# A two-block transformer kernel: output weights' loads put behind the input weights' loads, and the norm's transposes moved by one token tile

## The chip, the cores and the metric

The kernel runs on one core of a Trainium2 chip. Its engines are TensorE (PE, the matmuls), VectorE (DVE), ScalarE (ACT), GpSimd (POOL) and SyncE (SP, which here only issues loads); each works through its own instructions in order and waits for the others by semaphores. The metric is the device time of one execution in microseconds. "Faster" and "slower" are told from the median of several runs.

## The reference

The input is one sequence of 512 tokens of width 1024, in fp32. The first block has two layers: softmax attention with a forget gate, and then a differential attention on shared keys and values. Each is followed by a convolutional feed-forward part:

```python
def _conv_ffn(x, w_in, conv_w, conv_b, w_out):
    u = x @ w_in
    up = jnp.pad(u, ((0, 0), (CONV_WIDTH - 1, 0), (0, 0)))
    u = sum(conv_w[j] * up[:, j:j + s] for j in range(CONV_WIDTH)) + conv_b
    g, val = u[..., :D_FF], u[..., D_FF:]
    return (jax.nn.silu(g) * val) @ w_out
x = _layer_norm(DN_ALPHA * x + h, ...)       # after the attention
x = _layer_norm(DN_ALPHA * x + f, ...)       # after the feed-forward part
...
```

The second block normalises x (RMS norm), runs a grouped-query attention beside a state-space branch, mixes both through `w_out_2`, adds and normalises again, and ends with a gated feed-forward part of the same width (2816) and without the convolution: `(silu(gate) * up) @ w_down`.

## The kernel before

Every fp32 operand is split into a high and a low part, and each product is three matmuls (high x high, high x low, low x high). Tokens are held in four tiles of 128. A scheduler orders the instructions of each engine at build time; the order is fixed after that.

Weights come in chunks of 128 x 1024 (`wchunk`, L170): SP loads one (512 KB, L183) into one of three `raw` buffers, ACT makes the high part `whi` (L185), DVE the low part `wlo` (L186), each in one of four buffers.

The feed-forward part (`st_out`) runs three times: ffn0 (about 272 to 623 us), ffn1 (887 to 1250) and ffn2 (1738 to 2085). `w_in(g)` multiplies x by one group of input weights (four chunks), applies the convolution (L835, L837, L846) and the gate; `st_load` (L1403) loads four 512 KB pieces of output weights into `wr` buffers (L1410, five buffers); `st_phase` multiplies with them in the manner of Strassen. The loop is: load for phase g, `w_in(g + 2)`, phase g, `w_in(g + 3)`. While `w_in(1)` runs, the program also issues loads of constants for the stage that follows, on POOL's queue: in ffn0 four for the differential attention (`ropecos`, `ropesin`, `blockmask`, then `lam`), in ffn1 thirteen for the second block (L1039 to L1053, L168, L878). Small operations on these constants (L661, L663, L1041, L1047, L881) stand on DVE and ACT among the convolution's operations. In ffn2 there are none.

The last rows of the output weights are multiplied by `xs`, tile by tile; at each tile's end the epilogue does the residual and the norm (L390, L372 to L381; before the second block also L1596, L1600), and hands the transposes of the normed tile to `later`. `need(t - depth)` then emits those that are due. A transpose turns a tile in eight 128 x 128 steps (L330; after `w_out_2` L1510), and the result is split again into `xTh` (L193, ACT) and `xTl` (L194, DVE), the operands of the next stage. The three places where this happens are called A (end of ffn0, next the value projection of the differential attention), B (end of ffn1, next the keys and queries of the second block) and C (end of `w_out_2`, next ffn2). At C the norm's steps are L1341, L1347, L1349 and L1353, and the first products of ffn2 take 256 tokens at a time, so `need` asks for two tiles ahead of each half:

```python
            for t0 in (0, 256):
                self.need(t0 // P + 1)
                for i in range(2):
                    for p, c in zip(ps[i], (gc, vc)):
                        self.ws_mm(p, c, i * P, self.xh, self.xl, t0, t0 + 256)
```

Of the kernel before, what the change touches and what calls it, by code (L numbers as in the profile page):

```python
# [17 lines left out]
P = 128  # L18
# [62 lines left out]
class K:  # L81
# [90 lines left out]
    def wchunk(self, src):  # L172

        nc = self.nc
        srcs = src if isinstance(src, list) else [src]
        nk, cols = srcs[0].shape[0] // P, sum(a.shape[1] for a in srcs)
        assert nk * cols <= 1024
        raw = self.wp.tile([P, 1024], F32, tag="raw", name="raw", bufs=3)[:, :nk * cols]
        hi = self.wp.tile([P, 1024], F32R, tag="whi", name="whi", bufs=4)[:, :nk * cols]
        lo = self.wp.tile([P, 1024], F32R, tag="wlo", name="wlo", bufs=4)[:, :nk * cols]  # L180
        c = 0
        for a in srcs:
            nc.sync.dma_start(raw.rearrange("p (k c) -> p k c", k=nk)[:, :, c:c + a.shape[1]], a.rearrange("(k p) c -> p k c", p=P))  # L183
            c += a.shape[1]
        nc.scalar.activation(hi, raw, AF.Copy)  # L185
        nc.vector.tensor_tensor(out=lo, in0=raw, in1=hi.bitcast(F32), op=ALU.subtract)  # L186
        return hi.rearrange("p (k c) -> p k c", k=nk), lo.rearrange("p (k c) -> p k c", k=nk)
# [177 lines left out]

    def layer_norm(self, t, G, B, jk):

        nc = self.nc
        x = self.x[:, t, :]
        nm = self.sm.tile([P, 2], F32, tag="nm", name="nm")  # L370
        vs = self.sm.tile([P, 2], F32, tag="vs", name="vs")
        nc.vector.tensor_reduce(out=nm[:, 0:1], in_=self.sums[t][:, :self.ns], axis=AX.X, op=ALU.add)  # L372
        nc.vector.tensor_scalar(out=nm[:, 1:2], in0=nm[:, 0:1], scalar1=-1.0 / (32 * D), scalar2=None, op0=ALU.mult)
        for i in range(2):
            nc.scalar.activation(jk, x[:, i * 512:(i + 1) * 512], AF.Square, scale=1.0 / 32, bias=nm[:, 1:2], accum_out=vs[:, i:i + 1])
        nc.vector.tensor_scalar(out=nm[:, 0:1], in0=nm[:, 0:1], scalar1=-1.0 / D, scalar2=None, op0=ALU.mult)
        nc.vector.scalar_tensor_tensor(out=x, in0=x, scalar=nm[:, 0:1], in1=G, op0=ALU.add, op1=ALU.mult)
        r = self.rstd2(vs, LN_EPS)
        for i in range(2):
            h = slice(i * 512, (i + 1) * 512)  # L380
            nc.vector.scalar_tensor_tensor(out=x[:, h], in0=x[:, h], scalar=r, in1=B[:, h], op0=ALU.mult, op1=ALU.add)  # L381

# [31 lines left out]
    def fox(self, pool):  # L414
# [35 lines left out]
        def oproj(half, post=None):  # L450
            self.out_proj(I["a_w_out"][0], half * 4, 4, lambda k: oT[half * 4 + k][0], lambda k: oT[half * 4 + k][1],
                          1.0 if half else ALPHA, post)
# [32 lines left out]
        for h in range(17):  # L485
# [11 lines left out]
            if h == 15:  # L497
                oproj(0)
        G, B = self.bcast(I["ln_attn_g"][0], "Pt", pool, 1280, 2), self.bcast(I["ln_attn_b"][0], "Pt", pool, 1280, 2)
        oproj(1, self.norm_post(G, B, pool.tile([P, S], F32, tag="NC", name="NC")))  # L500

# [25 lines left out]
    def qk_stack1(self, qp, kp, pool, Ck, buf, e, scale=-0.125):  # L527
        nc = self.nc
        A = pool.tile([P, S], F32R, tag=f"A{e}", name="A", bufs=2)
        B = pool.tile([P, S], F32R, tag=f"B{e}", name="B", bufs=2)  # L530
        Cc = Ck[e][buf]
        m, o = (slice(0, 64), slice(64, 128)) if e == 0 else (slice(64, 128), slice(0, 64))
        nc.scalar.activation(A[m], qp[m], AF.Copy, scale=scale)
        nc.vector.scalar_tensor_tensor(out=A[o], in0=qp[m], scalar=scale, in1=A[m].bitcast(F32), op0=ALU.mult, op1=ALU.subtract)
        nc.scalar.activation(B[m], kp[m], AF.Copy)
        nc.scalar.activation(B[o], kp[m], AF.Copy)
# [695 lines left out]
    def block2(self, bpool):  # L1232
        nc, I, tc = self.nc, self.I, self.tc
        W = I["w_in_2"][0]
# [32 lines left out]
        with tc.tile_pool(name="L", bufs=self.NL) as self.L:  # L1267
# [31 lines left out]
            with tc.tile_pool(name="mix", bufs=1) as pool:  # L1299
# [6 lines left out]
                for t in range(NT):  # L1306
# [7 lines left out]
                    for g in range(2):  # L1314
# [4 lines left out]
                        k, s = slice(g * 4, g * 4 + 4), slice(t * P, (t + 1) * P)  # L1319
# [19 lines left out]
                def epi(c, t, ps):  # L1339
# [3 lines left out]
                    if c == 1:  # L1343
# [10 lines left out]
                        self.later(t, lambda: self.to_T2(mo[t], t))  # L1354
                        for i in range(2):
                            nc.gpsimd.dma_start(xd[t, i], x[t][i])
                self.depth = 1
                for c in range(2):
                    self.xs(I["w_out_2"][0], c * 512, 512, KD, lambda k: mx[k][0], lambda k: mx[k][1], lambda t, ps, c=c: epi(c, t, ps), stagger=4 if c else 0)
        with tc.tile_pool(name="ffn2", bufs=1) as pool:  # L1360
# [1 line left out]

    NL = 38
    F0 = 1
    depth = 1

    @staticmethod
    def steps(gen, n):
# [108 lines left out]
    def st_out(self, pool, W, x, fresh, w_in, last, WR=5):  # L1477

        hs = {}
        Q = [pool.tile([P, 2, 512], F32, tag="Q", name="Q", bufs=4) for _ in range(4)]  # L1480

        def group(g, R):
            if g < 8:
                hs[g] = self.st_operands(pool, R)
            else:
                hs[g] = [pool.tile([P, self.BLOCKS], F32R, tag=n, name=n, bufs=3)[:, :1024] for n in ("hh", "hl")]
                self.split(R[:, :1024], *hs[g])

        for g in range(2):
            group(g, w_in(g))  # L1490
        for g in range(0, 8, 2):
            B = self.st_load(pool, W, g, WR)
            R = w_in(g + 2)
            self.st_phase(pool, B, (hs[g], hs[g + 1]), Q, x, g == 0, fresh and g == 0, WR)
            group(g + 2, R)
            R = w_in(g + 3)
            if g == 6:
                self.st_final(Q, x, fresh)
            group(g + 3, R)
        group(10, w_in(10))  # L1500
        op = lambda i: lambda k: hs[8 + k // 2][i][:, k % 2 * 512:(k % 2 + 1) * 512]
        epis = last()
        for c in range(2):
            self.xs(W, c * 512, 512, 6, op(0), op(1), epis(c), k0=16, stagger=3 * c, banks=3 * (1 - c))
# [129 lines left out]
```

## Time and profile before

| | |
|---|---|
| median of 3 runs | 2103.84 us (2103.47 to 2104.33) |
| profiled execution | 2104.43 us |
| its span | 2102.6 us, so 1.8 us lie around it |
| granted TensorE clock, mean | 0.992 |
| busy: PE, DVE, ACT, POOL | 2045.3, 1556.9, 1085.2, 77.5 us |
| chain that ended last | PE 80%, DVE 7%, ACT 7%, issue 3%, POOL 2%, DMA 2% |

PE is busy for 97% of the span. Since a busy engine may run at a lower clock, the granted clock is read beside it: 1.00 is 2.4 GHz, 0.5 is 1.2 GHz, and a window that holds both shows a value between. An idle time in square brackets stands in front of the row that ended it, with the row or transfer that PE waited for.

### The profile page before, as it was taken

Reading aid. Unit: us, or ns where it says so; the run is one execution under the profiler, and the core shown is the slowest. Engines: PE = TensorE matmul, PEld = TensorE weight load, DVE = VectorE, ACT = ScalarE, POOL = GpSimd, SP = SyncE. Lnnn points to the kernel's source line nnn. Section 1 sums busy time; section 2 is a strip of 40 time slices with the busy share of each in tenths; the row PEclk is TensorE's granted clock in tenths of the full one; section 3 lists DMA queues with packets and bytes.
Section 4 is the critical chain, followed back from the end, with each engine's and each line's share of the span. In section 5 each row is a group of like instructions: output and inputs, shape, how many; then the busy total and the mean of one; then the engine's idle time right before and its main releaser. Section 6 shows DMA issues by size and latency. Waiting matters only on the chain.

```text
span 2102.6 us, 28049 instructions
## 1 busy us (share of the span) xinstructions
PE 2045.3 (97%) x10563; PEld 1729.3 (82%) x10563; DVE 1556.9 (74%) x2776; ACT 1085.2 (52%) x1905; POOL 77.5 (4%) x113
## 2 busy tenths in 40 slices
PE   8999999999999999999999999999999999999998
PEld 7888888888878789888888877877898878888886
DVE  6777878788966888767887867897798545575564
ACT  4777655444435977445444443677476334443322
POOL 0000000000000000110000002000000001000000
PEclk9999999999999999999999999999999999999999
DMA  6222243233223221153223323211323425333222
GB/s 169 62 61 61 71 138 103 78 101 120 83 88 91 61 78 53 58 145 110 80 91 110 110 91 96 68 32 44 106 59 88 145 90 191 101 100 99 82 80 90
DMA packets 197469, 193.71 MB, mean 92 GB/s; under 512 B 8933, under 2 KB 170454, under 8 KB 197334
## 3 DMA queue, kind: packets, MB, share of 16 engines
q1 hardware_dynamic: 191398, 173.04, 27.5%
q0 software_dynamic: 5504, 17.31, 2.8%
q8 instruction: 83, 1.36, 0.3%
q10 hardware_dynamic: 432, 1.57, 0.2%
q14 instruction: 52, 0.43, 0.1%
HBM read 185.61 MB, written 6.29 MB: 91 GB/s over the span
## 4 chain that ended last, share of the span: by engine, by line
PE 80%; DVE 7%; ACT 7%; issue 3%; POOL 2%; DMA 2%; POOLq 0%; DVEq 0%; SPq 0%; ACTq 0%
PE mm L219 15%; PE mm L217 15%; PE mm L218 15%; PE at L1439 3%; PE at L1440 3%; PE at L1438 3%; PE mm L291 3%; PE mm L293 3%; PE mm L292 3%; PE at L401 2%; ACT sw L699 1%; DVE wlo L186 1%; PE mm L257 1%; PE mm L259 1%; PE mm L258 1%
## 5 line engine op out<-in xcount | busy, mean ns | idle before, releaser
L217 PE MATMUL mm<-xTh,whi 128*128 128x512 f32 (+1 forms) x1584 | 606.9, 383 | 4.7 <-ACT whi L185 3.3
L219 PE MATMUL mm<-xTh,wlo 128*128 128x512 f32 (+1 forms) x1584 | 605.5, 383 | 2.6 <-DVE wlo L186 2.6
L218 PE MATMUL mm<-xTl,whi 128*128 128x512 f32 (+1 forms) x1584 | 605.3, 382 | 0.0
L185 ACT ACTIVATE whi<-raw 128x1024 fp32r<-128x1024 f32 (+3 forms) x282 | 293.0, 1043 | 311.0 <-PE mm L218 172.7
L186 DVE TENSOR_TENSOR wlo<-raw,whi 128x1024 fp32r<-128x1024 f32 (+3 forms) x282 | 337.2, 1199 | 141.5 <-ACT whi L185 135.6
L217 PEld LDWEIGHTS mm<-xTh,whi 128*128 128x128 f32 x1584 | 299.6, 189 | 60.2 <-ACT whi L185 3.7
L219 PEld LDWEIGHTS mm<-xTh,wlo 128*128 128x128 f32 x1584 | 299.2, 189 | 59.4 <-DVE wlo L186 3.7
L218 PEld LDWEIGHTS mm<-xTl,whi 128*128 128x128 f32 x1584 | 299.6, 189 | 55.2 <-DVE xTl L194 0.2
L837 DVE SCALAR_TENSOR_TENSOR cy<-mm,cols,cy 128x511 f32<-128x511 f32 (+1 forms) x172 | 128.3, 746 | 69.7 <-ACT cy L835 67.6
L193 ACT ACTIVATE whi<-wr 128x1024 fp32r<-128x1024 f32 x84 | 89.0, 1060 | 90.2 <-PE mm L218 29.1
L835 ACT ACTIVATE cy<-mm,cols 128x512 f32<-128x512 f32 x86 | 66.5, 773 | 105.5 <-PE mm L219 105.5
L291 PE MATMUL mm<-whi,xTh 128*128 128x256 f32 x416 | 119.0, 287 | 0.8 <-ACT xTh L193 0.5
L292 PE MATMUL mm<-wlo,xTh 128*128 128x256 f32 x416 | 118.5, 285 | 0.4 <-DVE wlo L186 0.4
L293 PE MATMUL mm<-whi,xTl 128*128 128x256 f32 x416 | 118.5, 285 | 0.2 <-DVE xTl L194 0.2
L194 DVE TENSOR_TENSOR wlo<-wr,whi 128x1024 fp32r<-128x1024 f32 x84 | 102.0, 1221 | 12.9 <-ACT whi L193 12.1
L193 ACT ACTIVATE hh<-R 128x256 fp32r<-128x256 f32 (+2 forms) x57 | 54.9, 964 | 82.9 <-DVE R L1528 42.3
L1439 PE MATMUL at<-wlo,hh 128*128 128x512 f32 x240 | 93.4, 389 | 0.0
L1440 PE MATMUL at<-whi,hl 128*128 128x512 f32 x240 | 93.4, 389 | 0.0
L1438 PE MATMUL at<-whi,hh 128*128 128x512 f32 x240 | 92.7, 389 | 0.0
L193 ACT ACTIVATE ph<-at 128x512 fp32r<-128x512 f32 (+3 forms) x128 | 58.7, 474 | 53.8 <-PE at L401 40.3
L291 PEld LDWEIGHTS mm<-whi,xTh 128*128 128x128 f32 x416 | 80.1, 193 | 2.3 <-ACT xTh L193 1.0
L292 PEld LDWEIGHTS mm<-wlo,xTh 128*128 128x128 f32 x416 | 80.3, 193 | 1.6 <-DVE wlo L186 0.6
(451 smaller groups left out, 3860.9 us busy)
## 6 DMA issues: line engine op xcount, KB each, us to landing
raw<-in_ffn_w_in_dram SPq DMA_DIRECT2D x88, 512.0 KB
raw<-in_w_gate_up_dram SPq DMA_DIRECT2D x44, 512.0 KB
raw<-in_w_in_dram SPq DMA_DIRECT2D x40, 512.0 KB
wr<-in_ffn_w_out_dram SPq DMA_DIRECT2D x32, 512.0 KB
raw<-in_a_w_in_dram SPq DMA_DIRECT2D x22, 512.0 KB
raw<-in_kv_w_dram SPq DMA_DIRECT2D x16, 512.0 KB
wr<-in_w_down_dram SPq DMA_DIRECT2D x16, 512.0 KB
raw<-in_ffn_w_out_dram SPq DMA_DIRECT2D x12, 512.0 KB
```

What stands on the lines that cost most here:

```text
L185: nc.scalar.activation(hi, raw, AF.Copy)
L186: nc.vector.tensor_tensor(out=lo, in0=raw, in1=hi.bitcast(F32), op=ALU.subtract)
L193: nc.scalar.activation(hi, src, AF.Copy)
L217: mm(o, wh, a, start=(k == 0), stop=False)
L218: mm(o, wh, b, start=False, stop=False)
L219: mm(o, wl, a, start=False, stop=(k == ktiles - 1))
L291: mm(o, a, hi[:, kk, :], start=(k == 0 and t % 2 == 0), stop=False)
L292: mm(o, a, lo[:, kk, :], start=False, stop=False)
L293: mm(o, b, hi[:, kk, :], start=False, stop=(k == ktiles - 1 and t % 2 == 1))
L1438: mm(ps[t], a, wh, start=p == 0, stop=False)
L1439: mm(ps[t], a, wl, start=False, stop=False)
L1440: mm(ps[t], b, wh, start=False, stop=p == 1)
```

## The change

It has two parts. `wchunk` keeps the load that it issued last, and the four loads of a phase's output weights are issued after it, so they stand behind the last chunk of the input weights asked for so far. And `depth` is 2 in place of 1, for all three places: the transposes of tile t come at the end of tile t + 2 in place of t + 1.

```diff
--- before.py
+++ after.py
@@ -180,7 +180,7 @@
         lo = self.wp.tile([P, 1024], F32R, tag="wlo", name="wlo", bufs=4)[:, :nk * cols]
         c = 0
         for a in srcs:
-            nc.sync.dma_start(raw.rearrange("p (k c) -> p k c", k=nk)[:, :, c:c + a.shape[1]], a.rearrange("(k p) c -> p k c", p=P))
+            self.last_load = nc.sync.dma_start(raw.rearrange("p (k c) -> p k c", k=nk)[:, :, c:c + a.shape[1]], a.rearrange("(k p) c -> p k c", p=P)).ins
             c += a.shape[1]
         nc.scalar.activation(hi, raw, AF.Copy)
         nc.vector.tensor_tensor(out=lo, in0=raw, in1=hi.bitcast(F32), op=ALU.subtract)
@@ -1354,7 +1354,6 @@
                         self.later(t, lambda: self.to_T2(mo[t], t))
                         for i in range(2):
                             nc.gpsimd.dma_start(xd[t, i], x[t][i])
-                self.depth = 1
                 for c in range(2):
                     self.xs(I["w_out_2"][0], c * 512, 512, KD, lambda k: mx[k][0], lambda k: mx[k][1], lambda t, ps, c=c: epi(c, t, ps), stagger=4 if c else 0)
         with tc.tile_pool(name="ffn2", bufs=1) as pool:
@@ -1362,7 +1361,7 @@
 
     NL = 38
     F0 = 1
-    depth = 1
+    depth = 2
 
     @staticmethod
     def steps(gen, n):
@@ -1489,7 +1488,8 @@
         for g in range(2):
             group(g, w_in(g))
         for g in range(0, 8, 2):
-            B = self.st_load(pool, W, g, WR)
+            with self.tc.issue_after(self.last_load):
+                B = self.st_load(pool, W, g, WR)
             R = w_in(g + 2)
             self.st_phase(pool, B, (hs[g], hs[g + 1]), Q, x, g == 0, fresh and g == 0, WR)
             group(g + 2, R)
```

The order of SP's loads at the beginning of ffn0, before (-) and after (+); `raw` holds input weights, `wr` output weights:

```order
 L183 DMA raw<-in_a_w_out_dram 128x2x512 x4
-L183 DMA raw<-in_ffn_w_in_dram 128x4x256 x7
-L1410 DMA wr<-in_ffn_w_out_dram 128x2x512 x4
 L183 DMA raw<-in_ffn_w_in_dram 128x4x256 x8
-L1410 DMA wr<-in_ffn_w_out_dram 128x2x512 x4
+L1409 DMA wr<-in_ffn_w_out_dram 128x2x512 x4
```

The eighth load of input weights, the last chunk of `w_in(1)`, now stands ahead of the first four of output weights (the line number of these moves by one); ffn1 and ffn2 change in the same way, and every later group as well.

The order on DVE at place B, from the second norm's scaling of tile 0 (L1600) on, before:

```order
L1600 SCALAR_TENSOR_TENSOR Q<-x,ss_11344,wr 128x512 x2
L377 SCALAR_TENSOR_TENSOR x<-x,nm,wr 128x1024
L1381 SCALAR_TENSOR_TENSOR ss_11377<-vs 128x1
L194 TENSOR_TENSOR xTl<-at,xTh 128x4x128
L381 SCALAR_TENSOR_TENSOR x<-x,ss_11378,wr 128x512 x2
L194 TENSOR_TENSOR xTl<-at,xTh 128x4x128
L1381 SCALAR_TENSOR_TENSOR ss_11388<-ss_11385 128x1
L1600 SCALAR_TENSOR_TENSOR Q<-x,ss_11389,wr 128x512 x2
L390 SCALAR_TENSOR_TENSOR x,sums<-x,at 128x512
```

and after:

```order
L1600 SCALAR_TENSOR_TENSOR Q<-x,ss_11344,wr 128x512 x2
L377 SCALAR_TENSOR_TENSOR x<-x,nm,wr 128x1024
L1380 SCALAR_TENSOR_TENSOR ss_11377<-vs 128x1
L390 SCALAR_TENSOR_TENSOR x,sums<-x,at 128x512
L381 SCALAR_TENSOR_TENSOR x<-x,ss_11378,wr 128x512 x2
L372 TENSOR_REDUCE nm<-sums 128x1
L194 TENSOR_TENSOR xTl<-at,xTh 128x4x128
L373 TENSOR_SCALAR nm<-nm 128x1
L194 TENSOR_TENSOR xTl<-at,xTh 128x4x128
```

L377 and L381 are the first norm of the next tile, L194 the splits of a transposed tile. Before, tile 0's two splits stood in front of tile 2's residual (L390); now this residual stands in front of the splits, and so on for the following tiles.

The order on ACT at place C, from the scaling of tile 1 (L1353, `ss_16113`) on, before:

```order
L1353 ACTIVATE L<-L,ss_16113 128x512 x2
L1341 ACTIVATE jk,ss_15860<-mm 128x512
L193 ACTIVATE xTh<-at 128x4x128 x2
L185 ACTIVATE whi<-raw 128x1024
```

and after:

```order
L1353 ACTIVATE L<-L,ss_16113 128x512 x2
L1341 ACTIVATE jk,ss_15860<-mm 128x512
L193 ACTIVATE xTh<-at 128x4x128 x2
L185 ACTIVATE whi<-raw 128x1024
L1349 ACTIVATE jk,ss_16152<-L 128x512
L185 ACTIVATE whi<-raw 128x1024
L1349 ACTIVATE jk,ss_16152<-L 128x512
L185 ACTIVATE whi<-raw 128x1024
L1353 ACTIVATE L<-L,ss_16162 128x512 x2
L1341 ACTIVATE jk,ss_15861<-at 128x512
L193 ACTIVATE xTh<-at 128x4x128 x2
```

The first L193 pair is the split of tile 1 before and of tile 0 after. After, tile 1's pair comes only behind the scaling of tile 2 (L1353, `ss_16162`) and the first norm step of tile 3 (L1341). On PE, where before tile 2's products, tile 1's transposes and tile 3's products followed each other, tile 3's products now come ahead of tile 1's transposes, and the first products of ffn2 right behind these.

## Rows read from the trace of the kernel before

**Rows 1.** The page: busy us (share of the span) xinstructions.

```profile
PE 2045.3 (97%) x10563; PEld 1729.3 (82%) x10563; DVE 1556.9 (74%) x2776; ACT 1085.2 (52%) x1905; POOL 77.5 (4%) x113
```

**Rows 2.** PE's waits, whole kernel: us in total, times, longest.

```profile
PE at L330 <- DVE x L381: 5.9, 10, 1.7
PE at L330 <- DVE Q L1600: 5.4, 2, 5.1
...
PE at L1510 <- ACT L L1353: 2.0, 2, 1.1
```

**Rows 3.** Timeline of PE, ffn0: start, duration, instruction [idle before <-releaser].

```profile
300.19 0.50 PE L217 MATMUL mm<-xTh,whi 128*128 128x512 f32 x1 [1.28 <-ACT whi L185]
...
301.95 0.79 PE L219 MATMUL mm<-xTh,wlo 128*128 128x512 f32 x1 [1.02 <-DVE wlo L186]
...
307.14 0.39 PE L219 MATMUL mm<-xTh,wlo 128*128 128x512 f32 x1
```

**Rows 4.** Timeline of PE, ffn1, the same place.

```profile
921.32 0.50 PE L217 MATMUL mm<-xTh,whi 128*128 128x512 f32 x1 [1.99 <-ACT whi L185]
...
923.60 0.79 PE L219 MATMUL mm<-xTh,wlo 128*128 128x512 f32 x1 [1.54 <-DVE wlo L186]
...
930.16 0.40 PE L219 MATMUL mm<-xTh,wlo 128*128 128x512 f32 x1
```

**Rows 5.** Windows: length; PE, PEld, DVE, ACT, POOL busy; clock, DMA share, GB/s.

```profile
288.00:290.00 2.00, 2.00 (x19) 2.00 (x19) 0.00 (x0) 0.00 (x0) 0.00 (x0) 1.00 1.05 414
300.00:304.00 4.00, 2.78 (x7) 1.96 (x8) 3.99 (x6) 3.68 (x6) 0.00 (x0) 0.70 0.21 54
362.00:371.00 9.00, 9.00 (x41) 7.48 (x40) 5.93 (x7) 2.12 (x2) 0.00 (x0) 1.00 0.73 226
625.00:640.00 15.00, 14.44 (x89) 12.61 (x87) 11.87 (x22) 7.00 (x14) 2.01 (x2) 1.00 0.24 68
924.00:930.00 6.00, 6.00 (x16) 4.64 (x16) 6.00 (x10) 2.77 (x4) 0.00 (x0) 0.53 0.34 95
1250.00:1254.00 4.00, 4.00 (x14) 3.51 (x14) 3.87 (x7) 1.94 (x5) 0.55 (x1) 0.51 0.00 0
```

**Rows 6.** Timeline of SP's loads, ffn0: first issue, time to the last.

```profile
283.89 1.91 SPq L1410 DMA_DIRECT2D wr<-in_ffn_w_out_dram  x4
...
361.77 28.30 SPq L183 DMA_DIRECT2D raw<-in_ffn_w_in_dram  x8
```

**Rows 7.** Timeline of POOL, ffn0: the last of the four loads of constants.

```profile
286.03 0.54 POOL L656 DMA_DIRECT2D lam<-in_b_lambda_dram  x1
```

**Rows 8.** Timeline of DVE, ffn0.

```profile
293.39 0.29 DVE L661 TENSOR_TENSOR lam<-lam 128x128 f32<-128x128 f32 x1 [7.50 <-DMA lam<-in_b_lambda_dram]
...
300.68 1.22 DVE L186 TENSOR_TENSOR wlo<-raw,whi 128x1024 fp32r<-128x1024 f32 x1
```

**Rows 9.** Timeline of ACT, ffn0.

```profile
294.09 0.20 ACT L663 ACTIVATE ls<-ls 128x2 f32<-128x2 f32 x1 [7.98 <-issue]
```

**Rows 10.** Timeline of POOL, ffn1: the last of the thirteen loads of constants.

```profile
915.94 0.54 POOL L878 DMA_DIRECT2D gaink<-in_k_norm_dram  x1 [0.51 <-DMA c_sums<-const_sums_dram]
```

**Rows 11.** Timeline of DVE, ffn1: the row that uses this last load.

```profile
920.00 0.43 DVE L881 TENSOR_TENSOR ctk<-c_axcos,gaink 128x256 f32<-128x256 f32 x1 [0.72 <-DMA gaink<-in_k_norm_dram]
```

**Rows 12.** Timeline of ACT, ffn0: first split of a later group.

```profile
379.19 1.07 ACT L185 ACTIVATE whi<-raw 128x1024 fp32r<-128x1024 f32 x1 [1.71 <-PE mm L218]
```

**Rows 13.** Timeline of PE, end of ffn0 (place A).

```profile
623.25 1.32 PE L330 MATMUL at<-ident,x 128*128 128x128 f32 x8 [1.67 <-DVE x L381]
```

**Rows 14.** Timeline of PE, end of ffn1 (place B).

```profile
1249.77 1.97 PE L330 MATMUL at<-ident,Q 128*128 128x128 f32 x8 [5.12 <-DVE Q L1600]
...
1285.83 1.99 PE L950 MATMUL at<-ident,L 128*128 128x128 f32 x8 [2.50 <-ACT L L923]
```

**Rows 15.** Timeline of PE, the first product of ffn2 (place C).

```profile
1738.61 0.28 PE L217 MATMUL mm<-xTh,whi 128*128 128x256 f32 x1
```

**Rows 16.** Timeline of ACT, end of w_out_2: the scaling of tile 2.

```profile
1740.68 1.34 ACT L1353 ACTIVATE L<-L,ss 128x512 f32<-128x512 f32 x2 [1.12 <-POOL ss L1382]
```

## The prediction

> **What bounds the kernel now.** I read the page first: the matmul engine is busy for nearly the whole span [rows 1], so only what it waits for, and what it runs at the lower clock, can be won. Next the table of its waits: among the longest groups are transposes of the norm's output that wait for the norm itself, on DVE (line L381, 5.9 us in 10 waits; L1600, 5.4 us in 2) and on ACT (L1353, 2.0 us in 2) [rows 2]. These are the ends of the first two feed-forward parts (ffn0, ffn1) and of w_out_2. Then the timelines at the waits that stand outside the norms: the two 1 to 2 us pairs where the second group of input weights begins in ffn0 and ffn1 [rows 3, 4]. Last the windows around each of these, for the granted clock [rows 5]: a pair of waits of 1.28 and 1.02 us is followed by a stretch at 0.70, one of 1.99 and 1.54 by 0.53 (16 matmuls in 6 us), one of 5.12 by 0.51; near 0.5 is the lower of the engine's two levels, 1.2 in place of 2.4 GHz. A full-clock 512-column matmul starts every 0.227 us, and a 256-column one every 0.12.
>
> **Part 1, the loads.** In ffn0 the four output-weight loads (4 x 512 KB) go out at 283.89, and the constants (3 x 256 KB, then 128 KB of lam) are issued from POOL, the last at 286.03 [rows 6, 7]. The window 288 to 290 shows the DMA engines full at 414 GB/s [rows 5]. lam lands at about 293.3: DVE's L661 waits 7.50 for it and starts at 293.39 [rows 8], ACT's L663 then at 294.09 after 7.98 idle [rows 9]. 3.0 MB at 414 GB/s are 7.3 us, so the transfer itself is the whole of that wait. Behind them, in order on both engines, stand the convolution of the first group (L835, L837, a table load, L846) and then the splits of the next weights: L186 begins at 300.68 and takes 1.22 [rows 8], and PE waits 1.28 and 1.02 for the two halves of that split [rows 3]. After the change the fourth load of this group of input weights stands ahead of the output weights. It needs a buffer that the first split frees, so all 2 MB leave the stretch of the constants. What is left is 0.9 MB, 2.2 us at that rate, so lam could land near 288.5; a gain vector of ffn1, issued at 915.94 when less is in flight, is used at 920.00 [rows 10, 11], some 4 us later, by which lam lands at 290. The sums that the convolution reads are complete at about 290.1 (24 matmuls of 0.12 from 287.2, where the second half of that product starts), so the convolution starts at 290.4 in place of 294.2, 3.8 us sooner, and the split ends near 298.1, before the previous group's last matmul (298.76). PE then runs 22 matmuls of 0.227 from 298.8 and comes to the third product of the second chunk at 303.8 in place of 307.14 [rows 3]: **-3.3 us**. The split of that chunk stands at most 5.2 behind the first one (301.95 to 307.14), so it is there at 303.3, just in time. Bounds: 0 if lam lands no sooner, and -4.0 if both waits and the lower clock (1.7) go.
>
> In ffn1 the same happens with 13 constants. POOL itself waits there: from the ninth on each issue waits until one eight before has landed, the last goes out at 915.94 [rows 10], and the DVE row that needs it, L881, starts at 920.00 after waiting 0.72 [rows 11]; L186 ends just before 923.60, where PE gets it [rows 4]. The earlier ones land after 6 to 9 us, this last one, with the output weights through, after 4; with 4 to 5 for all of them the chain of issues ends some 3.5 us sooner, and L881 can begin at 916; L186 then ends at 919.5. PE's waits of 1.99 and 1.54 and the stretch at 0.53 go [rows 4, 5]; 22 matmuls from 919.2 reach the second chunk's third product at 924.2, its split, 5 us behind the first, allows 924.5, and before it was 930.16 [rows 4]: **-5.5 us**, between 0 and -6.9 (both waits, and half of a lower-clock stretch of 6.8). In the third part (ffn2) no constants are loaded at that place and PE shows no such wait: 0.
>
> The rule of the Trainium skill, "DMA: Bandwidth & Descriptors", section "Queues, rings and completion order", says that each DMA engine takes turns between the queues that have work, packet by packet. By it the constants would have had half of the rate beside the output weights and lam would have landed at about 290.6, where the row has 293.3; by it only some 2 us are to be won in ffn0, and the sum would be 1.2 us smaller. The row shows no such half share, and I go by the row.
>
> What part 1 might cost: the output weights of a phase go out later, by 18 us in ffn0 (they wait for the buffer freed at 301.9). They are first used after a whole further group of input weights, about 40 us on. In the later groups the order is one load of input weights, 2 MB of output weights, then the next input weights: those were issued from 361.77 on [rows 6], and the first of them is split only at 379.19 [rows 12]. 3.1 MB within 17.4 us asks for 181 GB/s; the stretch from 362 to 371 moved 226 at a DMA share of 0.73 [rows 5]. The cover is these 17 us; cost 0, and if it failed, a few us for each of nine groups.
>
> **Part 2, the transposes two tiles later.** No instruction is added. A tile's 8 transposes stand behind one more tile of products on PE (24 or 18 matmuls), and its two splits behind one more tile's norm on DVE and ACT.
>
> Place A, ffn0 into the value projection: PE waits 1.67 at 623.25 for the first tile's norm [rows 13], 2.6 over the place (the L381 row of the whole kernel is 5.9 [rows 2]). The 18 matmuls now ahead (4.1 us) cover the first wait. But DVE is busy for 11.9 of 15 us there [rows 5], and the later splits come later: I follow it to three small waits of 1.3 us together, fewer transposes in pieces, and the value projection's end at 658.1 in place of 661.0 with the following waits counted; I take **-2.5**, between +1 and -3.
>
> Place B, ffn1 into the second block: the norm's two stages (L381, then L1600) leave PE idle for 5.12 us, and 14 matmuls then take 4 us at 0.51 [rows 5, 14]: 5.1 plus about 2. Now tile 2's products (4.1 us) go ahead, which leaves 1.2 of the wait and no lower clock. New waits: 0.8 for the second split of tile 1, and 1.5 for tile 2's behind tile 3's norm. 7.1 - 1.2 - 0.8 - 1.5 = 3.6, and the transposes at L950 that ended on ACT with a wait of 2.50 at 1285.83 [rows 14] start near 1281.8: **-4**, between +2 and -7.
>
> Place C, w_out_2 into ffn2: here the wait that goes is only 1.1 us. The first products of ffn2 take columns 0 to 255, so they need tiles 0 and 1 both. Before, tile 3's last products stood between tile 1's transposes and these, which began at 1738.61 [rows 15]. Now tile 3's products are done first (end near 1735.7), tile 1 is transposed by 1736.6, and its split on ACT stands behind the scaling of tile 2 (L1353 at 1740.68 [rows 16]) and the first norm step of tile 3: it ends near 1742.3. PE idles 5.7 us. The later waits of 0.9 and 0.3 shrink or stay; ffn2's first group ends 3.0 us later. To this comes the lower clock, which the 5.12 us wait of place B brought on for about 2 us; I count half: **+4**, between 0 (if ACT's queue runs ahead) and +7.7.
>
> The Trainium skill, "TensorE: Matmul & The Clock Gate", section on the HAM clock gate, has it that the half rate is the default state and that activity releases it. By that rule the idle at C always costs the lower clock and C is +5, the sum 1 us smaller. The 5.12 us row agrees; that C idles so long no row shows yet.
>
> **Sum.** -3.3 - 5.5 - 2.5 - 4 + 4 = -11.3 us on the profiled execution's 2104.43 (span 2102.6 and 1.8 around it): 2093.1. The median of the runs is 2103.84, 0.6 below it, so **2092.5**.
>
> **Rivals.**
> 1. The constants land no sooner, since POOL's own issue (0.54 us each, and the wait for eight) paces them. For it: the 13 issues of ffn1 [rows 10]. Against it: in ffn0 only four are issued, with no wait. Then -2.5 - 4 + 4 = -2.5, 2101.3.
> 2. The transposes gain nothing at A and B, because DVE and ACT, not PE's order, set the pace there. For it: DVE's 11.9 of 15 us. Against: the window of B, where DVE idles before L1600. Then -8.8 + 4, 2099.0.
> 3. C costs nothing, since ACT comes to tile 1's split in time: -15.3, 2088.5. Against it is ACT's order.
> 4. Slower: the way from a tile's transposes to its second split, now behind one more norm, is longer than the products in between. At A and B these are one tile's 36 products of 0.12, 4.3 us; the mechanism decides from a way of over 4.3 us on, where the wait before the first transposes stays as well. Each place then pays what the row at B shows, 5.1 and 2 of lower clock: 7.1 at A and B each, 6 at C, against -8.8 of part 1: +11.4, 2115.
>
> **Chances.** Forecast 0.60, rival 1 0.10, rival 2 0.13, rival 3 0.10, rival 4 0.07. Range 2085 to 2102: it takes in the forecast's own bounds (about 2087 to 2098) and rivals 1 to 3. By 0.2% (4.2 us, about what a measurement of this kernel can tell from no change): faster 0.75 (the forecast, rival 3, half of rival 2), same 0.18 (rival 1, half of rival 2, a little of the forecast), slower 0.07.
>
> **What the profile after would show.** Part 1: L661 of ffn0 starting by 290.5 and the two waits at L217 and L219 gone in ffn0 and ffn1, with a granted clock of 1.00 there; if L661 still waits 7 us, rival 1 holds. Part 2: at A no wait before the first tile's transposes; at B a wait of 1 to 1.5 us in place of 5.12; at C a wait of 5 to 6 us of L217 for ACT's or DVE's split of xTh or xTl, which the kernel before does not have. If C shows none, rival 3; if A or B shows waits of 4 us and more for xTh or xTl, rival 4. Waits of L217 for raw loads in the later groups of an ffn would say that the 17 us of cover were not there.

## The result and the profile after

The changed kernel took 2091.99 us in the median of 4 runs (2091.34 to 2092.55), against 2103.65 (2102.65 to 2104.33, 4 runs) before: 11.66 us less, a ratio of 0.9943 with a 95% interval of 0.9930 to 0.9955. The profiled execution took 2091.34 us with a span of 2089.6.

Both traces have 10563 matmul rows, in the same order outside the three places, so the n-th matmul of one can be set against the n-th of the other. Its start in the changed kernel less its start before, taken ahead of and behind each place, gives what the place won or lost:

```
place                       predicted   measured
ffn0, second input group      -3.3       -4.24
A, end of ffn0                -2.5       -3.71
ffn1, second input group      -5.5       -5.11
B, end of ffn1                -4.0       -4.25
C, start of ffn2              +4.0       +3.59
sum                          -11.3      -13.72
```

B is read up to the end of w_out_2's products, since stretches at the lower clock in the second block shift with its start. The rest of the program moved by 0.13 us or less at any landmark, but for 0.65 us at its very start. The last matmul comes 13.07 us earlier. The medians differ by less, since the profiled execution before was 0.8 above its median and the one after 0.7 below. C is read at 1745 us of the kernel before; another 0.1 us is lost there up to 1770.

PE's waits after, over the whole kernel, in the columns of [rows 2]:

```profile
PE mm L217 <- ACT xTh L193: 5.6, 2, 5.3
PE at L330 <- DVE x L381: 3.4, 7, 0.8
...
PE at L950 <- ACT L L923: 2.4, 1, 2.4
...
PE mm L219 <- DVE wlo L186: 1.2, 2, 0.8
...
PE at L330 <- DVE Q L1600: 0.9, 1, 0.9
```

The wait of 5.1 us for L1600 is 0.9, the wait of L1510 for L1353 is gone from the table, and a new one stands there, L217 for tile 1's split (L193), with 5.3 us in one piece. (An entry is the waiting line and what ended the wait.)

**The loads.** The same stretch of ffn0 after, rows of SP's queue, POOL, DVE and ACT (start, duration, instruction, idle before):

```profile
271.55 27.65 SPq L183 DMA_DIRECT2D raw<-in_ffn_w_in_dram  x5
299.41 1.91 SPq L1409 DMA_DIRECT2D wr<-in_ffn_w_out_dram  x4
```

```profile
286.57 0.54 POOL L656 DMA_DIRECT2D lam<-in_b_lambda_dram  x1
```

```profile
290.29 0.29 DVE L661 TENSOR_TENSOR lam<-lam 128x128 f32<-128x128 f32 x1 [3.87 <-DMA lam<-in_b_lambda_dram]
...
297.58 1.22 DVE L186 TENSOR_TENSOR wlo<-raw,whi 128x1024 fp32r<-128x1024 f32 x1
```

```profile
290.98 0.20 ACT L663 ACTIVATE ls<-ls 128x2 f32<-128x2 f32 x1 [4.34 <-issue]
```

SP now issues the fifth input load (it waits for the buffer, so the row is long) and only then, at 299.41, the output weights, where [rows 6] has 283.89. lam is issued at 286.57 and used 3.7 us later, not 7.4 as in [rows 7, 8]; ACT's idle time of 7.98 [rows 9] is 4.34. The first split L186 starts at 297.58 instead of 300.68. PE has no wait here, so nothing answers to the first two of [rows 3], and the window has a full clock where [rows 5] has 0.70:

```profile
300.00:304.00 4.00, 4.00 (x19) 3.30 (x18) 4.00 (x8) 2.28 (x3) 0.00 (x0) 1.00 0.96 330
```

In ffn1, POOL, DVE and PE:

```profile
897.38 0.60 POOL L1039 DMA_DIRECT2D dtb<-in_dt_bias_f_dram  x1 [2.08 <-PE at L330]
...
903.26 0.59 POOL L878 DMA_DIRECT2D gainq<-in_q_norm_dram  x1
903.78 0.59 POOL L878 DMA_DIRECT2D gaink<-in_k_norm_dram  x1
```

```profile
908.69 0.42 DVE L881 TENSOR_TENSOR ctq<-c_axcos,gainq 128x256 f32<-128x256 f32 x1 [3.04 <-DMA gainq<-in_q_norm_dram]
...
911.89 1.21 DVE L186 TENSOR_TENSOR wlo<-raw,whi 128x1024 fp32r<-128x1024 f32 x1
```

```profile
913.16 0.50 PE L219 MATMUL mm<-xTh,wlo 128*128 128x512 f32 x1 [0.79 <-DVE wlo L186]
...
918.20 0.50 PE L219 MATMUL mm<-xTh,wlo 128*128 128x512 f32 x1 [0.43 <-DVE wlo L186]
```

The last constant is issued at 903.78, 6.4 us after the first; before, POOL waited between issues and needed 11.1 us for them [rows 10]. What is late now is gainq, issued at 903.26 and used at 908.69. Of PE's two waits of [rows 4] one is left, 0.79 us long, and a new one of 0.43 stands at the split of the next chunk.

**The transposes.** PE at the three places, in this order: A, B (two pieces, from 1237.06), C:

```profile
621.83 1.04 PE L330 MATMUL at<-ident,x 128*128 128x128 f32 x8
```

```profile
1237.06 1.32 PE L330 MATMUL at<-ident,Q 128*128 128x128 f32 x8 [0.86 <-DVE Q L1600]
...
1247.81 0.39 PE L293 MATMUL mm<-whi,xTl 128*128 128x256 f32 x1 [0.74 <-DVE xTl L194]
```

```profile
1259.01 0.39 PE L291 MATMUL mm<-whi,xTh 128*128 128x256 f32 x1 [1.09 <-ACT xTh L193]
...
1269.09 0.91 PE L950 MATMUL at<-ident,L 128*128 128x128 f32 x4 [2.35 <-ACT L L923]
```

```profile
1718.90 1.03 PE L1510 MATMUL at<-ident,L 128*128 128x128 f32 x8
1725.25 0.98 PE L217 MATMUL mm<-xTh,whi 128*128 128x256 f32 x3 [5.31 <-ACT xTh L193]
```

At A the first tile's transposes start without a wait ([rows 13] has 1.67). At B they wait 0.86 instead of 5.12 [rows 14], with small new waits for splits of 0.74 and 1.09; the wait of L950 stays at 2.35. At C the first products of ffn2 wait 5.31 us. The windows at A, at B (behind the first tile's wait, as in [rows 5]), and at C (the idle part and what follows it) show DVE's share and the clock:

```profile
622.00:637.00 15.00, 14.85 (x107) 13.69 (x106) 14.18 (x27) 8.36 (x17) 1.35 (x3) 1.00 0.29 78
1237.00:1241.00 4.00, 3.94 (x21) 3.19 (x22) 3.88 (x9) 2.40 (x5) 0.55 (x1) 1.00 0.03 10
1720.00:1725.30 5.30, 0.05 (x1) 0.06 (x1) 5.17 (x7) 4.45 (x10) 1.55 (x2) 1.00 0.55 191
1725.30:1728.70 3.40, 3.40 (x16) 3.40 (x17) 3.27 (x7) 2.77 (x6) 1.67 (x3) 0.50 1.01 320
```

At B the lower clock of [rows 5] is gone; at C there are 3.4 us of it, at 1.2 GHz, behind the idle time. ACT and DVE say why PE waited at C:

```profile
1722.80 1.33 ACT L1353 ACTIVATE L<-L,ss 128x512 f32<-128x512 f32 x2 [0.85 <-POOL ss L1381]
1724.04 0.57 ACT L1341 ACTIVATE jk<-at 128x512 f32<-128x512 f32 x1
...
1724.61 1.07 ACT L193 ACTIVATE xTh<-at 128x512 fp32r<-128x512 f32 x2
```

```profile
1721.12 3.50 DVE L186 TENSOR_TENSOR wlo<-raw,whi 128x1024 fp32r<-128x1024 f32 x3
...
1725.41 0.68 DVE L194 TENSOR_TENSOR xTl<-at,xTh 128x512 fp32r<-128x512 f32 x1
...
1728.77 0.68 DVE L194 TENSOR_TENSOR xTl<-at,xTh 128x512 fp32r<-128x512 f32 x1
```

Tile 1 was transposed by 1719.9. Its split (L193, 1724.61) stood on ACT behind tile 2's scaling (L1353, which itself waited for POOL) and tile 3's L1341, the order that [rows 16] and the order of ACT's instructions had announced. DVE splits tile 1 in two halves; the second (1728.77) stands behind tile 3's norm (L1347, L1350) and is a second thing that comes late at C.

### The profile page after: what moved, and what is told of

Its sections match the earlier page's. It is cut to its first block, busy times and chain, and to the rows that moved or that the text cites. A ratio compares the mean times of both kernels' runs of the same rounds, so it can differ in the third digit from the quotient of the medians.

```text
span 2089.6 us, 28051 instructions
## 1 busy us (share of the span) xinstructions
PE 2038.2 (98%) x10563; PEld 1724.7 (83%) x10563; DVE 1554.7 (74%) x2776; ACT 1085.3 (52%) x1905; POOL 75.6 (4%) x113
## 4 chain that ended last, share of the span: by engine, by line
PE 80%; DVE 8%; ACT 7%; issue 3%; POOL 1%; DMA 1%; POOLq 0%; DVEq 0%; ACTq 0%; SPq 0%
PE mm L219 15%; PE mm L218 15%; PE mm L217 15%; PE mm L293 3%; PE mm L291 3%; PE mm L292 3%; PE at L1437 3%; PE at L1438 3%; PE at L1439 3%; PE at L401 2%; DVE wlo L186 1%; ACT sw L699 1%; PE mm L1437 1%; PE mm L1438 1%; PE mm L1439 1%
## 5 line engine op out<-in xcount | busy, mean ns | idle before, releaser
L217 PE MATMUL mm<-xTh,whi 128*128 128x512 f32 (+1 forms) x1584 | 605.4, 383 | 8.2 <-ACT xTh L193 5.6
L186 DVE TENSOR_TENSOR wlo<-raw,whi 128x1024 fp32r<-128x1024 f32 (+3 forms) x282 | 337.1, 1199 | 146.0 <-ACT whi L185 140.2
L217 PEld LDWEIGHTS mm<-xTh,whi 128*128 128x128 f32 x1584 | 298.9, 189 | 63.3 <-ACT xTh L193 6.1
L193 ACT ACTIVATE whi<-wr 128x1024 fp32r<-128x1024 f32 x84 | 89.0, 1060 | 90.2 <-PE mm L218 29.1
L194 DVE TENSOR_TENSOR wlo<-wr,whi 128x1024 fp32r<-128x1024 f32 x84 | 101.9, 1220 | 12.9 <-ACT whi L193 12.0
L193 ACT ACTIVATE hh<-R 128x256 fp32r<-128x256 f32 (+2 forms) x57 | 54.9, 963 | 85.4 <-DVE R L1528 43.2
L193 ACT ACTIVATE ph<-at 128x512 fp32r<-128x512 f32 (+3 forms) x128 | 58.6, 474 | 54.2 <-PE at L401 40.7
L293 PEld LDWEIGHTS mm<-whi,xTl 128*128 128x128 f32 x416 | 80.2, 193 | 3.4 <-DVE xTl L194 1.9
```

Of the source, the lines that this page charges most:

```text
L193: nc.scalar.activation(hi, src, AF.Copy)
L217: mm(o, wh, a, start=(k == 0), stop=False)
L293: mm(o, b, hi[:, kk, :], start=False, stop=(k == ktiles - 1 and t % 2 == 1))
```

## Experiments

What each place won or lost, read from each trace as above (us, against the kernel before), and the medians with their interval to the kernel before on the same chip. Edits are shown against the changed kernel unless said otherwise, cut to the lines that matter:

```
kernel                 ffn0     A    ffn1     B      C    median   ratio, 95% interval
changed               -4.24  -3.71  -5.11  -4.25  +3.59  2091.99  0.9943 [0.9930, 0.9955]
e1 loads only         -4.25  +0.05  -5.97  +0.07  +0.01  2095.46  0.9961 [0.9946, 0.9976]
e2 transposes only    +0.03  -3.69  +0.72  -3.96  +3.84  2100.60  0.9985 [0.9976, 0.9994]
e3 one tile at C      -4.06  -3.69  -5.83  -4.17  +0.01  2087.10  0.9923 [0.9909, 0.9938]
e4 half a tile at C   -4.25  -3.69  -5.85  -4.10  +1.01  2088.11  0.9929 [0.9912, 0.9945]
e5 half of the loads  -2.36  -3.69  -4.84  -4.05  +3.69  2093.63  0.9949 [0.9934, 0.9964]
e6 first phase only   -4.23  -3.69  -5.61  -4.26  +0.01  2087.73  0.9919 [0.9902, 0.9935]
e7 POOL scales at C   -4.25  -3.69  -5.81  -4.18  +3.38  2091.51  0.9938 [0.9923, 0.9953]
e8 a third at A, B    -3.99  -3.78  -5.85  -3.54  +0.01  2087.78  0.9921 [0.9906, 0.9936]
e9 filled idle at C   -4.25  -3.71  -6.00  -4.27  +4.61  2093.15  0.9944 [0.9931, 0.9959]
e10 three tiles A, B  -4.07  +1.74  -6.01  -0.75  -0.01  2093.75  0.9947 [0.9931, 0.9964]
```

With the same instructions at a place the runs repeat within 0.3 us at ffn0, A, B and C, but gave -5.1 to -6.0 in ffn1, so a difference of 1 us there is not read as an effect. Every one of these traces comes to ffn0 0.5 to 1.6 us later than the trace of before, and e5, e6 and e9 lose another 0.8 to 1.2 us near 700 us, where nothing was edited. The kernel before took 2103.47 us beside e1 to e4, 2105.40 beside e5 to e8 and 2104.06 beside e9 and e10, so a difference of up to 2 us between medians of different groups says nothing; there the places decide.

**e1, the loads alone.**

```diff
-    depth = 2
+    depth = 1
```

> Only the loads' order is changed; the transposes stay one tile later as before. Theory (the two parts add up place by place): ffn0 -4.2 and ffn1 -5.1 us as in the changed kernel's trace, A, B and C as before: 9.3 below the kernel before, 2094.3. Rival (the earlier input weights are what A and B gained from, not the transposes' place): A and B gain here too, -17, 2086.5.

2095.46, 8.0 below the kernel before and 1.2 above the theory; its trace comes to ffn0 1.2 us late. A and B gained nothing, both starts of the second input group their full share.

**e2, the transposes alone.** The loads are issued as before; the edit is against the kernel before:

```diff
-                self.depth = 1
+                self.depth = 2
-    depth = 1
+    depth = 2
```

> Only the transposes are moved; the loads stand as before. Theory: A -3.7, B -4.2, C +3.6: 4.3 below the kernel before, 2099.4, and the two waits at the start of the second input group in ffn0 and ffn1 are there as before. Rival (A and B gain by the loads): only C's loss is left, +3.6, 2107.

2100.60, 2.9 below the kernel before, where the theory had 4.3, with a spread from 2097.45 to 2102.42 in 10 runs. Places A, B and C have their terms; the two waits at the second input group are back. Together e1 and e2 settle which part owns which place, and that the parts add up: 8.0 and 2.9 are 10.9, against 11.7 for both.

**e3, back to one tile at C.**

```diff
+                self.depth = 1
                 for c in range(2):
```

> As the changed kernel, but with the transposes one tile later at the end of w_out_2 as before. Theory: C's +3.6 is given back and nothing else moves: 16.7 to 17.3 below the kernel before, 2086.5 to 2087. Rival (what C loses is compensated later, as ffn2 has slack elsewhere): no gain, 2092.

2087.10: the theory's number, 4.9 us below the changed kernel, of which 3.6 are read at C, and 16.4 below the one before. This is the best version of all runs, together with e6 and e8, which can't be told from it.

**e4, half a tile earlier at C.** In `xs`, for this place only:

```diff
-            for ch in last:
+            for i, ch in enumerate(last):
                 part(t, ch)
+                if self.half and i == len(last) // 2 - 1:
+                    self.need(t - 2)
```

> As the changed kernel, but at the end of w_out_2 tile t's transposes stand behind half of tile t+2's products, so tile 1's behind half of tile 3's. Theory (at C only the lateness of tile 1's split costs, the wait of 1.1 us before tile 0's transposes is gone by then): C is 0 to 2 us better than before, 2085 to 2087. Rival (at C any transposes later than one tile push the splits behind the norm on ACT, and DVE and ACT pace it): C still loses 2 us or more against before, 2089 to 2092.

2088.11, C +1.01: neither. The wait before tile 0's transposes is gone, but 2.17 us before the first product of ffn2 are left, and 3.4 us at the lower clock follow. PE in e4 (line numbers shifted by 4):

```profile
1716.11 1.03 PE L1514 MATMUL at<-ident,L 128*128 128x128 f32 x8
...
1722.06 0.38 PE L217 MATMUL mm<-xTh,whi 128*128 128x256 f32 x1 [2.17 <-ACT xTh L193]
```

So a later place is a loss at C even by half a tile, while the wait it removes was only 1.1 us.

**e5, half of the output weights early.** In `st_load`:

```diff
-            self.nc.sync.dma_start(B[i, j].rearrange("p (g c) -> p g c", g=2), Wv[i, j][:, g:g + 2, :])
+            with self.tc.issue_after(self.last_load) if g or i else nullcontext():
+                self.nc.sync.dma_start(B[i, j].rearrange("p (g c) -> p g c", g=2), Wv[i, j][:, g:g + 2, :])
```

> As the changed kernel, but at the first phase of each feed-forward part two of the four output-weight loads stay ahead of the last load of the second input group, as in the kernel before, and two go behind it: 1 MB instead of 2 or none beside the constants. Theory (bytes in flight beside the constants hold these back): lam lands half way, DVE's wait at L661 in ffn0 is 5.5 to 6 us (7.5 before, 3.9 in the changed kernel), about half of the 4.2 and 5.1 us is lost, 2096 to 2097. Rival (what pays is the order itself, that the last input-weight load stands first in its queue): it stands between the halves and so behind half the loads still, nothing of 9.3 is won, 2101. Rival (the constants' own latency): no loss, 2092.

2093.63, where the theory had 2096 to 2097. In ffn0 it is the theory's dose: DVE waits 5.79 for lam, between 7.50 and 3.87, and the place keeps 2.36 of 4.24 us.

```profile
292.44 0.29 DVE L662 TENSOR_TENSOR lam<-lam 128x128 f32<-128x128 f32 x1 [5.79 <-DMA lam<-in_b_lambda_dram]
```

Both rivals fall with this in ffn0: something is won, and something is lost. In ffn1 the dose did not show in PE's time: -4.84. POOL's issues are half way there too (first to last 8.5 us, against 6.4 and 11.1), but the last ones then land faster (gainq is used 3.6 us after its issue, 5.4 in the changed kernel), and the split L186 ends only 0.3 us later than in the changed kernel, counted from the end of the group before. By this place the expected number was missed; why the last landings differ was not tried.

**e6, only the first phase reordered,** otherwise e3:

```diff
-            with self.tc.issue_after(self.last_load):
+            with self.tc.issue_after(self.last_load) if g == 0 else nullcontext():
```

> Transposes as in e3 (one tile later at the end of w_out_2, two elsewhere); the loads are reordered at the first phase of each feed-forward part only, the three later phases stand as in the kernel before. Theory (the gain is all at the constants): as e3, 2087.1 within 1.5. Rival (the later groups' order has a price or a gain of its own, some tenths at each of nine places): 2 us or more away from e3.

2087.73, as e3. The nine later groups neither gain nor pay: between 320 and 612 us of ffn0, where three of them lie, both traces move by 0.03 us against the kernel before.

**e7, tile 2's scaling on POOL at C.**

```diff
+                            if t == 2:
+                                nc.gpsimd.tensor_scalar(out=mo[t][i], in0=mo[t][i], scalar1=r, scalar2=None, op0=ALU.mult)
+                            else:
                                 nc.scalar.activation(mo[t][i], mo[t][i], AF.Copy, scale=r)
```

> As the changed kernel, but at the end of w_out_2 the scaling of tile 2 (two instructions of L1353) is done by POOL, so that tile 1's split stands ahead of nothing but L1341 on ACT. Theory (ACT's order makes PE idle 5.3 us at place C): PE's wait there falls to 2.5 to 3.5 us, 1.5 to 3 us of C's 3.6 come back, 2089 to 2090.5. Rival (DVE's queue, where three weight splits L186 stand ahead of tile 1's second split, is as late): PE's wait only moves to the next product, 2092.

2091.51, C +3.38. PE's wait did fall, from 5.31 to 3.14, as ACT's order has it, and DVE's first split of tile 1 moved up with it (1724.03, 1725.41 in the changed kernel). But nothing came of it, and the time is the rival's: the two scalings take POOL 3.60 us (1.34 on ACT), tile 2's transposes wait for them, tile 3's norm on DVE waits 2.29 us for POOL's L1384, which stands behind them, and tile 1's second split, behind this norm, starts at 1729.54 in place of 1728.77. The stretch at the lower clock is 6.8 us long here, from 1722.9 on. PE, POOL, DVE and the window in e7:

```profile
1723.02 1.01 PE L217 MATMUL mm<-xTh,whi 128*128 128x256 f32 x3 [3.14 <-ACT xTh L193]
...
1724.94 1.11 PE L1513 MATMUL at<-ident,L 128*128 128x128 f32 x4 [0.69 <-POOL L L1354]
```

```profile
1722.83 3.60 POOL L1354 TENSOR_SCALAR L<-L,ss 128x512 f32<-128x512 f32 x2
```

```profile
1727.00 1.42 DVE L1347 SCALAR_TENSOR_TENSOR L<-L,ss 128x512 f32<-128x512 f32 x2 [2.29 <-POOL ss L1384]
...
1729.54 0.68 DVE L194 TENSOR_TENSOR xTl<-at,xTh 128x512 fp32r<-128x512 f32 x1
```

```profile
1723.00:1729.70 6.70, 5.99 (x27) 5.69 (x28) 4.41 (x9) 2.91 (x6) 5.14 (x5) 0.50 0.58 187
```

That the wait stands behind ACT's order is shown. C's loss is not this wait alone: DVE's second split came no sooner, which is the rival's account, though PE, at the lower clock, shows no wait for it here.

**e8, a third of a tile at A and B,** otherwise e3: the edit of e4, on at A and B:

```diff
+    half = True
+                self.depth, self.half = 1, False
                 for c in range(2):
```

> Best version so far (e3), with tile t's transposes at places A and B behind a third of tile t+2's products (6 of 18 matmuls) in place of all of them. Theory (at A and B what is left are waits for splits that come late, 2 to 3 us at B): 1 to 2 us better than e3, 2085 to 2086. Rival (then PE waits for the norm before the first transposes again: at B these came 0.9 us late even behind all 18): B loses 2 to 3 us, 2089 to 2090.

2087.78, as e3: A -3.78, B -3.54. Neither: B pays 0.6 us, not 2 to 3 (two waits for L1600 of 1.5 us together, one of 0.9 in e3).

**e9, PE's idle time at C filled.**

```diff
                 self.need(t0 // P + 1)
+                if self.fill and t0 == 0:
+                    for j in range(40):
+                        self.nc.tensor.transpose(ps[0][0][:, j % 4 * P:j % 4 * P + P], self.ident, self.ident)
```

> As the changed kernel, but 40 transposes of a constant (4.4 us), whose result is overwritten, fill PE's 5.3 us idle at place C. Theory (of C's 3.6 us about 1.7 is the lower clock that follows the idle time): no stretch at 0.50 after it, C +1.9, 2090.3. Rival (the products at the lower clock wait for the next tiles' splits anyway, so it costs nothing): C +3.6, 2092.

2093.15, C +4.61 (read with the 40 added rows counted off). PE and DVE in e9, and the window behind the filling:

```profile
1720.08 4.53 PE L229 MATMUL mm<-ident 128*128 128x128 f32 x40
...
1726.45 0.38 PE L218 MATMUL mm<-xTl,whi 128*128 128x256 f32 x1 [0.52 <-DVE xTl L194]
...
1729.87 0.39 PE L218 MATMUL mm<-xTl,whi 128*128 128x256 f32 x1 [1.49 <-DVE xTl L194]
```

```profile
1729.13 0.68 DVE L194 TENSOR_TENSOR xTl<-at,xTh 128x512 fp32r<-128x512 f32 x1
```

```profile
1725.00:1729.00 4.00, 2.31 (x15) 1.91 (x15) 3.83 (x7) 3.38 (x8) 1.67 (x3) 1.00 0.91 300
```

The clock stays at 1.00, and the time is not better: PE now waits 0.52 and 1.49 us for DVE's xTl, the second time for the second split of tile 1, which starts as late as in the changed kernel. There PE does not wait for it: with its products at the lower clock, and four of tile 2's transposes among them, it comes to this split only when it is there. The theory that 1.7 us of C are the lower clock falls. The order of tile 2's transposes moved as well in this kernel, so the 1.0 us by which it is worse is not explained further. That the lower clock is free only up to this split fits three kernels with the same instructions at C: products ran at 0.50 for 3.4 us in the changed kernel, 3.6 in e5 and 4.0 in e2, and C reads +3.59, +3.69 and +3.84.

**e10, three tiles at A and B,** otherwise e3:

```diff
-    depth = 2
+    depth = 3
```

> As e3 (one tile later at place C), with the transposes at A and B three tiles later in place of two. Theory (the splits queue behind one more norm on DVE and ACT, as at C): at A and B PE has no products of other tiles left to do before the first split, so it idles 3 to 6 us at each: 5 to 12 us worse than e3, 2092 to 2099. Rival (what is left at B are waits for the norm, which one more tile covers): 1 us better than e3, 2086.

2093.75, 6.7 us worse than e3, inside the theory's range. At A PE waits 2.74 us for a split it did not wait for at two tiles, and 6.8 us at the lower clock follow (PE, and the window):

```profile
632.31 0.58 PE L293 MATMUL mm<-whi,xTl 128*128 128x256 f32 x1 [2.74 <-DVE xTl L194]
```

```profile
631.10:637.90 6.80, 5.59 (x26) 5.59 (x27) 6.73 (x14) 1.63 (x4) 1.10 (x2) 0.50 0.47 136
```

The idle is less than the theory's 3 to 6 us at each place: 3.0 at A, and at B the waits sum to 0.4 more than in e3. What else A and B lose against e3 (5.4 and 3.4 us in all) stands with the lower clock, 6.8 us of it at A and 10.2 at B (from 1248.9 on).

## Why the prediction was right

The forecast of 2092.5 met 2091.99, by the forecast's mechanism at every place but for how the loads share the DMA engines, with errors of size that partly cancel. That it came within 0.5 us is in part luck: the places won 13.7 us where 11.3 were forecast, and the later start of the trace after (0.65) and the distance of the two profiled executions from their medians (0.8 and 0.7) took most of the difference back. ffn0 and A lie outside their own bounds (-4.0 and -3). The bounds of "about 2087 to 2098" are not the places' bounds added up, which give about 2083 to 2114.

- ffn0: lam's landing was forecast for 288.5 to 290 and DVE's L661 for 290.4; it started at 290.29, and 0.5 us of that is the later start of the run. The wrong size, -3.3 for -4.24, is a miscount: between PE's first wait and the row at 307.14 there are 18 matmuls and not 22, 0.9 us too many.
- ffn1: -5.5 for -5.11. The chain of issues ended 4.7 us sooner (3.5 forecast, both on the time scale of before), but gainq's landing came later than the 4 to 5 us assumed (5.4 from issue to use), and waits of 0.79 and 0.43 stayed. Here too the 22 matmuls are 18, and the 0.9 us too many happened to stand for the wait of 0.79. Rival 1 falls with both places, and POOL's wait between issues is a consequence of slow landings, not a pace of its own.
- That the bytes beside the constants hold them back is shown by e5 in ffn0: from its issue to its use lam took 7.4 us beside 2.1 MB, 5.6 beside 1.05 MB and 3.7 beside none. How they do it the forecast had wrong: it took the transfer of all 3.0 MB for the whole of the wait and saw no half share. The DMA views show two parts (q0 carries POOL's loads, q1 SP's; packets, MB, share of the engines). Before, from 283 to 288 us, then from 288 to 293:

```profile
q1 hardware_dynamic: 480, 0.94, 56.3%
```

```profile
q0 software_dynamic: 288, 0.92, 56.1%
q1 hardware_dynamic: 466, 0.89, 47.2%
```

  After, from 286 to 290:

```profile
q0 software_dynamic: 288, 0.92, 75.6%
```

  Before, no byte of a constant moves until 288.1, 3.7 us after the first issue (284.38); then both queues move about as much, and the constants take 4.9 us. After, the first bytes move at 286.2, 1.3 us after the first issue (284.92), and they take 3.7 us. So 2.4 us of lam's 3.6 come from the earlier start and 1.2 from not sharing. With 1.05 MB in e5 the start is 3.5 us after the first issue, nearly as late as with 2.1 MB, and the transfer takes 3.3; in ffn1 the first bytes move 3.7 (before), 1.3 (after) and 3.5 us (e5) after the first issue. Why loads of SP make POOL's start late no run here shows. The rule of the Trainium skill, "DMA: Bandwidth & Descriptors", section "Queues, rings and completion order", is that each DMA engine takes turns between the queues with work; the trace before agrees from 288.1 on (0.92 and 0.89 MB). By it the output weights would delay the constants by no more bytes than these have themselves, 0.9 MB or 2.2 us as an estimate at 414 GB/s; sharing cost 1.2, and the late start is not in the rule.
- A: -2.5 for -3.71. The first wait went as forecast; the three small waits I had replayed for DVE did not come, there is no wait in PE's table over 610 to 662. DVE was the busy engine (14.18 of 15 us in 622 to 637), yet not late. Rival 2 falls at A and at B, by e2.
- B: -4 for -4.25: wait 0.86 (1.2 forecast), new waits 0.74 and 1.09 (0.8 and 1.5), no lower clock.
- C: +4 for +3.59: idle 5.31 us (5.7), clock at 0.50 behind it. That I counted half of 2 us for the clock is not borne out by e9. ACT's order is only part of the account: e7 shortened its wait by 2.2 us, and C only fell to +3.38. Tile 1's second split on DVE, which the forecast did not count, came no sooner there, and in e9 PE waits for it; what C costs with that split early was not tried. The rule of the Trainium skill, "TensorE: Matmul & The Clock Gate", section on the HAM clock gate, that the half rate is the default state and activity releases it, agrees with both traces (0.50 after the idle time, 1.00 in e9, where it was filled); the +5 that the forecast drew from it for C did not come. Rival 3 falls.
- Rival 4 (a way longer than the products in between) is what e10 shows one tile further: at three tiles A turns from -3.7 to +1.7 and B from -4.2 to -0.8. Its point of decision lies between two and three tiles at A, and at C between one and one and a half.
- What part 1 might have cost was put at 0, and e6 has it at 0.

## What to carry over

A transpose moved later pays only while other products stand between it and the first product that needs its split; count the norm work that its split then queues behind, place by place, and choose the distance for each place by itself (here two, two and one: by the medians 4.9 us better than two everywhere, 3.6 of them at C). A large prefetch with tens of microseconds of slack can sit in front of small loads that something waits for: let it go behind them. And a wait that is filled or moved to another engine is not won until the next wait behind it is looked at: at C two engines' splits came late, and easing one of them won 0.2 us.

## What the runs showed of the hardware

On POOL, the multiplication of a 128x512 fp32 tile by a per-row scalar took 1.8 us (3.60 for two), on ACT 0.67. From the ninth of POOL's loads on, an issue waited for the landing of the one eight before; with 2 MB less in flight the same thirteen were issued in 6.4 us with no wait, at some 0.53 us each. The first bytes of POOL's loads moved 1.3 us after the first issue with nothing of SP's in flight, and 3.5 to 3.7 us after it with 1.05 or 2.1 MB of SP's loads issued just before, in ffn0 and in ffn1; once they moved in ffn0, the two queues shared about evenly (0.92 and 0.89 MB in 5 us). Behind the idle time at C, holding the clock at 1.00 won nothing (e9), since the products then waited for their operands.
